# Norm weights and adaLN shifts applied along rows, and splits of four chunks out of PSUM, in a fused transformer kernel

## Chip, cores and metric

One Trainium2 chip, one core. The time is device microseconds of one execution, median of several. Lower is better.

## What is computed

512 tokens of width 1024 in float32 pass through two layers of a first block (a sparse-attention mixer "NSA", an MLP, a sliding-window mixer "SWA", a second MLP, each with adaptive norm) and then through a second block (a hybrid mixer, cross-attention to 256 memory tokens, a convolutional FFN). The parts that matter here are the norms in front of each of these and how their results enter the next projection:

```python
def modulate(h, shift, scale):
    return h * (1 + scale[:, None, :]) + shift[:, None, :]

mod = cond @ ada_w[i] + ada_b[i]
sh1, sc1, g1, sh2, sc2, g2 = jnp.split(mod, 6, axis=-1)
h = modulate(rms_norm(x, norm_g[i, 0]), sh1, sc1)      # mixer input
y = nsa_mixer(h, ...) or swa_sink_mixer(h, ...)
x = x + (1 + g1)[:, None, :] * rms_norm(y, norm_g[i, 1])
h = modulate(rms_norm(x, norm_g[i, 2]), sh2, sc2)      # MLP input
y = squared_relu_mlp(h, ...)
x = x + (1 + g2)[:, None, :] * rms_norm(y, norm_g[i, 3])
# second block: plain weights, no shift
h = rms_norm_2(x, norm_mix_w);   x = x + hybrid_mixer(h, ...)
h = rms_norm_2(x, norm_xattn_w); m = rms_norm_2(mem, norm_mem_w)
x = x + memory_cross_attention(h, m, ...)
h = rms_norm_2(x, norm_ffn_w);   x = x + conv_ffn(h, ...)
return rms_norm_2(x, norm_final_w)
```

So six times a normed and weighted x becomes the h of the next stage, three times (after NSA, the first MLP and SWA) with a shift, three times (after the second MLP, the hybrid mixer and cross-attention) without; the memory's norm is the seventh, and is done twice, since its keys and its values are made at different times.

## The kernel before

Matmuls keep float32 accuracy by three products of reduced-precision parts: `mm3` (L127) adds high by high, high by low and low by high. Every operand therefore exists as a high part, which ACT makes by a copy (`split`, L96), and a low part, which DVE makes by subtraction (L97). Weights come from HBM in 512 KB pieces through SP's queue (`load`, L77, in program order), into three buffers `st`, and `wload` (L113) splits each into `wh` and `wl` (five buffers each). The adaLN matrices are loaded by the same queue as tiles `ad` and multiplied on DVE (L341); when the eight jobs of one part are done, `ada_part` finishes its coefficient [128, 8], eight columns of 128 features (L357 for shifts, L363 for scales).

x lies with tokens on the partitions, four blocks of 128. The matmuls need h with features on the partitions: eight chunks of 128 features by 512 tokens. `norm_T` (L296) makes it. For each token block DVE multiplies the first half of x by the reciprocal norm r (L300) and ACT the second half (L301); TensorE transposes the eight 128 x 128 pieces (L448) into a PSUM bank "t"; for each chunk ACT (L315 without shift, L317 with) or DVE (L319, L321) takes it out of PSUM with the chunk's weight and shift as one scalar per partition, into a tile `nt`; then it is split into hH (ACT) and hL (DVE). `NB` gives the engine of each bank. h has eight tiles hH and eight tiles hL of [128, 512]; the same buffers carry the last attention outputs (`h_tile`), which the out-projection reads, and then the new h.

`norm_T` is called by `y_last` (after an out-projection with adaLN: NSA, first MLP, SWA, second MLP), by `to_h` (after those without) and by `mem_norm` (memory). In `y_last` a gate row `cb` is multiplied along the row (L931, L933 and the like); such a row comes from `along_rows` (L324): a coefficient [128, 8] is stored by POOL's DMA queue to a 4 KB tile Rd in DRAM with features in order (L327), then read back as a broadcast to 128 partitions (L329). There are five of these: the four gates and the final norm's weight.

The order of instructions is set by a planner over the program: each engine has one in-order stream, in which work is placed when its data are expected. Only the loads of `load` are held to program order.

Of the kernel before, what the change touches and what calls it, by code (L numbers as in the profile page):

```python
# [18 lines left out]
NST, NXT, NXQ, NAT = 6, 4, 4, 8  # L19
NAD, NR = 1, 3  # L20
NW = 5
TSE = 'GG'
NB = 'AVAV'
ON_PE = (8, 0, 1, 10, 3, 5)
FIRST = 5
XB, XE = ("mm", "t"), "AVAVAVAV"
# [19 lines left out]
def body(nc, tc, A, out):  # L46
# [89 lines left out]

    def chunk_terms(w, h, cols, ks):
        wh, wl = w
        hh, hl = h
        return [(kc(wh, j), kc(wl, j), hh[k][:, cols], hl[k][:, cols]) for j, k in enumerate(ks)]  # L140

    def h_tile():
        return [hp.tile([128, 512], F32R, name=n, tag=n, bufs=8) for n in ("hH", "hL")]

    def new_h(n=512, pool_=None, tags=("hH", "hL"), bufs=8):
        p_ = hp if pool_ is None else pool_
        hh = [p_.tile([128, n], F32R, name=tags[0], tag=tags[0], bufs=bufs) for _ in range(8)]
        hl = [p_.tile([128, n], F32R, name=tags[1], tag=tags[1], bufs=bufs) for _ in range(8)]
        return hh, hl

    def late_order(nk, n):

# [142 lines left out]

    def norm_T(xs, Rs, to, h, c, a, b=None):  # L296

        w = 128 * len(xs)
        for x, r, t in zip(xs, Rs, to):
            V.tensor_scalar(t[:, :512], x[:, :512], r, None, op0=OP.mult)  # L300
            S.activation(t[:, 512:], x[:, 512:], AF.Copy, scale=r)  # L301
        nb = 512 // w
        for m0 in range(0, 8, nb):
            o = mm("t")
            for u in range(nb):
                for i, t in enumerate(to):
                    transpose(o[:, u * w + i * 128:u * w + i * 128 + 128], kc(t, m0 + u))
            on = NB[m0 // nb]
            for u in range(nb):
                m = m0 + u  # L310
                hh, hl, v, g = h[0][m][:, c], h[1][m][:, c], kc(o, u, w), a[:, m:m + 1]
                t = tmp("nt", [128, 256], bufs=4)[:, :w]
                if on == "A":
                    if b is None:
                        S.activation(t, v, AF.Copy, scale=g)  # L315
                    else:
                        S.activation(t, v, AF.Identity, bias=b[:, m:m + 1], scale=g)  # L317
                elif b is None:
                    V.tensor_scalar(t, v, g, None, op0=OP.mult)  # L319
                else:  # L320
                    V.tensor_scalar(t, v, g, b[:, m:m + 1], op0=OP.mult, op1=OP.add)  # L321
                split(hh, hl, t)

    def along_rows(col, t):  # L324

        d = dr.tile([8, 128], F32, name="Rd", tag="Rd", bufs=2)
        G.dma_start(d.rearrange("m p -> p m"), col)  # L327
        flat = d.rearrange("m p -> (m p)")
        G.dma_start(t, bass.AP(tensor=flat.tensor, offset=flat.offset, ap=[[0, 128], [1, 1024]]))  # L329
        return t  # L330


    nw = {n: w2nd[:, 8 * i:8 * i + 8] for i, n in enumerate(("mix", "xattn", "mem", "ffn", "final"))}
    mod = C("mod", [128, 96])

    ada_pool = [None, 1, "ad"]
# [46 lines left out]
    def mem_norm(p, mh):  # L383
        ts, rs = [], []
        for i in range(2):
            t = p.tile([128, 1024], F32, name="relu", tag="relu", bufs=NR)
            Q.dma_start(t, A["mem"][i])
            ss = tmp("ss", [128, 4], bufs=12)
            mean_sq(t, ss[:, :1])
            ts.append(t)  # L390
            rs.append(rcol(ss[:, :1], 1))
        norm_T(ts, rs, ts, mh, slice(0, 256), nw["mem"])

    def mem_keys(p, mh):
        for m in range(8):
# [161 lines left out]
    def nsa(h, a_out):  # L557
        full = slice(0, 512)
        with ExitStack() as pools:
# [238 lines left out]
            def attend(i, g2, a):  # L798
# [24 lines left out]
                if a == 1:  # L823
                    two(O[g2], [VC[:, 2 * g2 + u] for u in range(2)], (qs[i][1],) * 2, False, True)
                if a == 1 and i == 3:
                    hh, ll = h_tile()
                    split(hh, ll, O[g2])
                    a_out[0].append(hh)
                    a_out[1].append(ll)
                elif a == 1:  # L830
                    oo = p5.tile([128, 512], F32, name="oo", tag="oo", bufs=2)
                    S.activation(oo, O[g2], AF.Copy)
                    Q.dma_start(Od[i * 2 + g2], oo)
# [87 lines left out]
    def y_last(how, src, a, nk, y, acc, x, h, cb, an, bn):  # L921

        ss = [small4() for _ in range(4)]

        def evac(tb, n, o):
            c = WIDTHS[n]
            if not acc:
                mean_sq(o, ss[tb][:, n:n + 1])
                V.tensor_tensor(y[:, tb, c], o, cb[:, c], op=OP.mult)  # L929
            else:  # L930
                V.tensor_tensor(y[:, tb, c], y[:, tb, c], o, op=OP.add)  # L931
                mean_sq(y[:, tb, c], ss[tb][:, n:n + 1])
                V.tensor_tensor(y[:, tb, c], y[:, tb, c], cb[:, c], op=OP.mult)  # L933

        def done(tbs):
            s2 = []
            for tb in tbs:
                r = total(ss[tb])
                s2.append(small4())
                for n, c in enumerate(WIDTHS):  # L940
                    V.scalar_tensor_tensor(x[:, tb, c], y[:, tb, c], r, x[:, tb, c], op0=OP.mult, op1=OP.add)
                    mean_sq(x[:, tb, c], s2[-1][:, n:n + 1])
            norm_T([x[:, tb] for tb in tbs], [total(s) for s in s2], [y[:, tb] for tb in tbs], h, cols_of(tbs), an(), bn())
        how(src, a, nk, evac, done)

    def x_last(src, a, nk, x, then):
# [166 lines left out]
    def mlp(l, h, p, pa, x, y, hn, an, bn, mem):  # L1113
        for tb in range(4):
            G.dma_start(Xd[tb], x[:, tb])
        with ExitStack() as pools:
            for g in range(4):
# [4 lines left out]
                if g == 3:  # L1122
                    seven_ctx.close()
                    for tb in range(4):
                        G.dma_start(x[:, tb], Xd[tb])
                    cb = along_rows(need(l, 5), pools.enter_context(pool("along")).tile(
                        [128, 1024], F32, name="along", tag="along"))
                blocks = Blocks(pa, sp) if g in (1, 2) else None

                def src7(k, n, q, g=g):  # L1130
# [65 lines left out]
    def swa(h, p, pa, a_out):  # L1196
# [24 lines left out]
        def attend(j, q2):  # L1221
# [4 lines left out]
            for jj in range(0, 4, 2):  # L1226
# [14 lines left out]
                for k in (jj, jj + 1):  # L1241
                    n = 256 if k < 3 else 128
                    for u in range(2):
                        T.matmul(O[64 * u:64 * u + 64, 128 * k:128 * k + n], VV[:, k, j // 2],
                                 pt[u][:, 256 * (k - jj):256 * (k - jj) + n], start=k == 0, stop=k == 3,
                                 skip_group_check=True)
            hh, ll = a_tile(pa, 6) if j < 3 else h_tile()
            split(hh, ll, O)
            a_out[0].append(hh)
            a_out[1].append(ll)  # L1250
# [65 lines left out]
    def hybrid(h, p, pa, a_out):  # L1316
# [142 lines left out]
                outs[hd] = ob  # L1459

        def combine(hd):
            hh, ll = a_tile(pa, 7) if hd < 3 else h_tile()
            G.tensor_tensor(outs[hd], outs[hd], gate[hd], op=OP.mult)
            split(hh, ll, outs[hd])
            a_out[0][4 + hd], a_out[1][4 + hd] = hh, ll
# [28 lines left out]
    def cross(h, p, pa, a_out):  # L1494
# [12 lines left out]
        def attend(hd):  # L1507
# [30 lines left out]
            for dc in range(2):  # L1538
                o = mm("o")
                mm3(o, [(kc(vv[j][0], 2 * hd + dc), kc(vv[j][1], 2 * hd + dc), pt[j][0], pt[j][1]) for j in range(2)])  # L1540
                hh, ll = a_tile(pa, 6) if hd < 3 else h_tile()
                split(hh, ll, o)
                a_out[0].append(hh)
                a_out[1].append(ll)
# [66 lines left out]
    def whole():  # L1611
# [7 lines left out]
        x = xp.tile([128, 4, 1024], F32, name="x", tag="x")  # L1619

        def to_h(hn, w):
            return lambda tbs, rs: norm_T([x[:, tb] for tb in tbs], rs, [tmp("xn", [128, 1024], bufs=4) for _ in tbs],
                                          hn, cols_of(tbs), w)

        def out_of(name):
# [207 lines left out]
```

## Time and profile before

| | us |
|---|---|
| median of three runs | 2063.8 (2063.65 to 2072.12) |
| the profiled execution | 2068.99 |
| its span in the profile | 2067.2 |
| TensorE busy | 1970.3 (95%) |
| DVE busy | 1351.1 (65%) |
| ACT busy | 971.9 (47%) |
| POOL busy | 295.4 (14%) |

The span runs from the first to the last instruction that the profile shows. Busy shares are means over stages of very different kinds; the mean granted clock of TensorE is 0.977 of full speed. A row of a view of groups gives line, engine, operation, output and inputs by name, the count, busy time, the mean duration, and the idle time of the engine just ahead of it with what ended it. A row of waits gives who waited, for what, and how long. All instants are microseconds from the start of the span.

### The profile page before, as it was taken

To read this page: it belongs to the slowest core of one execution; us is meant where nothing else is said; L and a number is where in the kernel's file an instruction comes from. 1 tells how busy PE (TensorE), PEld (TensorE's weight loads), DVE (VectorE), ACT (ScalarE), POOL (GpSimd) and SP (SyncE) were. 2 spreads that over 40 slices of the span, in tenths; PEclk is the share of its full clock that TensorE was granted. 3 is DMA by queue.
4 is the path that set the end of the run, shared out by engine and by line. 5 is a ranking of instruction groups with operands and counts; after the bars stand their busy time and mean duration, and the time that the engine had idled before them with its cause. 6 is when DMAs were issued, how large, how long until landed. Compare 5 with 4: busy or idle time off the path is not lost.

```text
span 2067.2 us, 27292 instructions
## 1 busy us (share of the span) xinstructions
PE 1970.3 (95%) x9878; PEld 1600.6 (77%) x9878; DVE 1351.1 (65%) x2608; ACT 971.9 (47%) x1846; POOL 295.4 (14%) x251
## 2 busy tenths in 40 slices
PE   8979999989989998999889999999999999999998
PEld 7766565678767887876678888888888888788786
DVE  6768777386677776776652676367635656767854
ACT  5346566363243434655543444455535454444442
POOL 0401211012022120320020211202010000301200
PEclk9999999999999999999989999999999999999999
DMA  7765331356935475540422343333322333252331
GB/s 296 227 191 152 102 114 49 112 195 205 273 122 174 166 240 147 171 135 20 173 93 92 117 148 123 133 112 117 98 72 68 106 114 107 85 155 92 102 103 51
DMA packets 89224, 276.64 MB, mean 134 GB/s; under 512 B 14209, under 2 KB 17217, under 8 KB 89090
## 3 DMA queue, kind: packets, MB, share of 16 engines
q1 hardware_dynamic: 82802, 258.68, 39.4%
q0 software_dynamic: 4432, 13.63, 2.0%
q10 hardware_dynamic: 1856, 2.59, 0.5%
q8 instruction: 78, 1.28, 0.3%
q14 instruction: 56, 0.46, 0.1%
HBM read 246.58 MB, written 10.51 MB: 124 GB/s over the span
## 4 chain that ended last, share of the span: by engine, by line
PE 44%; DVE 3%; ACT 1%; DMA 1%; issue 1%; POOL 0%; DVEq 0%; POOLq 0%; ACTq 0%
PE mm L130 10%; PE mm L131 10%; PE mm L132 10%; PE o L130 3%; PE o L132 3%; PE o L131 3%; DVE wl L97 1%; PE t L130 1%; PE t L131 1%; PE t L132 1%; PE t L448 1%; DMA st<-in_w_xq_dram 0%; ACT wh L96 0%; PE o L1445 0%; DMA st<-in_w_fdown_dram 0%
## 5 line engine op out<-in xcount | busy, mean ns | idle before, releaser
L130 PE MATMUL mm<-hH,wh 128*128 128x512 f32 (+1 forms) x1456 | 519.9, 360 | 22.3 <-ACT wh L96 14.1
L131 PE MATMUL mm<-hL,wh 128*128 128x512 f32 (+1 forms) x1456 | 520.8, 359 | 2.1 <-DVE hL L97 2.1
L97 DVE TENSOR_TENSOR wl<-st,wh 128x1024 fp32r<-128x1024 f32 x287 | 360.7, 1261 | 247.4 <-ACT wh L96 246.9
L132 PE MATMUL mm<-hH,wl 128*128 128x512 f32 (+1 forms) x1456 | 519.6, 359 | 2.4 <-DVE wl L97 2.4
L96 ACT ACTIVATE wh<-st 128x1024 fp32r<-128x1024 f32 (+1 forms) x295 | 308.7, 1052 | 447.8 <-PE mm L131 197.4
L130 PEld LDWEIGHTS mm<-hH,wh 128*128 128x128 f32 x1456 | 277.9, 192 | 63.9 <-ACT wh L96 15.1
L131 PEld LDWEIGHTS mm<-hL,wh 128*128 128x128 f32 x1456 | 279.0, 192 | 41.4 <-DVE hL L97 2.5
L132 PEld LDWEIGHTS mm<-hH,wl 128*128 128x128 f32 x1456 | 278.6, 192 | 41.7 <-DVE wl L97 3.0
L341 DVE SCALAR_TENSOR_TENSOR ad<-ad,cs 128x1024 f32<-128x1024 f32 x90 | 114.8, 1279 | 74.0 <-DMA ad<-in_ada_w_dram 73.7
L130 PE MATMUL o<-wh,aH 128*128 128x512 f32 x284 | 113.2, 399 | 10.0 <-DVE y L929 5.7
L130 PE MATMUL mm<-wh,aH 128*128 128x512 f32 x300 | 118.2, 396 | 4.0 <-ACT aH L96 4.0
L131 PE MATMUL mm<-wl,aH 128*128 128x512 f32 x300 | 118.5, 395 | 0.0
L132 PE MATMUL mm<-wh,aL 128*128 128x512 f32 x300 | 115.4, 393 | 0.0
L132 PE MATMUL o<-wh,aL 128*128 128x512 f32 x284 | 112.7, 397 | 0.5 <-DVE aL L97 0.5
L131 PE MATMUL o<-wl,aH 128*128 128x512 f32 x284 | 112.5, 396 | 0.0
L448 PEld LDWEIGHTS t<-pack,P 128*128 128x128 f32 x436 | 47.9, 143 | 63.4 <-issue 48.7
L1141 POOL TENSOR_TENSOR relu<-relu 128x512 f32<-128x512 f32 x32 | 54.7, 1711 | 277.7 <-ACT relu L1140 211.6
L448 PE MATMUL t<-pack,P 128*128 128x128 f32 x436 | 77.3, 292 | 10.6 <-ACT P L692 8.1
L753 ACT ACTIVATE P<-P,m 128x128 f32<-128x128 f32 (+3 forms) x128 | 70.9, 556 | 28.8 <-DVE m L751 27.3
L764 PE MATMUL o<-PT,VV 128*64 128x512 f32 (+3 forms) x256 | 79.3, 454 | 0.1
L96 ACT ACTIVATE aH<-relu 128x256 fp32r<-128x256 f32 (+2 forms) x70 | 41.4, 593 | 80.4 <-POOL relu L1150 43.0
L1150 POOL TENSOR_TENSOR relu<-relu 128x256 f32<-128x256 f32 (+1 forms) x46 | 57.2, 1254 | 146.6 <-ACT relu L1149 126.3
(467 smaller groups left out, 3651.9 us busy)
## 6 DMA issues: line engine op xcount, KB each, us to landing
ad<-in_ada_w_dram SPq DMA_DIRECT2D x90, 512.0 KB, 4.8
st<-in_w_up_dram SPq DMA_DIRECT2D x64, 512.0 KB, 3.6
st<-in_w_down_dram SPq DMA_DIRECT2D x56, 512.0 KB, 3.6
st<-in_w_fup_dram SPq DMA_DIRECT2D x44, 512.0 KB, 3.6
st<-in_w_fdown_dram SPq DMA_DIRECT2D x22, 512.0 KB, 3.5
st<-in_w_nsa_dram SPq DMA_DIRECT2D x16, 512.0 KB, 6.3
x<-in_w_down_dram SPq DMA_DIRECT2D x16, 512.0 KB, 3.9
raw<-in_w_down_dram SPq DMA_DIRECT2D x16, 512.0 KB, 3.8
```

The costliest lines, as they stand in the source:

```text
L96: S.activation(h, src, AF.Copy)
L97: eng.tensor_tensor(l, src, f(h), op=OP.subtract)
L130: T.matmul(o, ah, bh, start=start and i == 0, stop=False, **kw)
L131: T.matmul(o, ah, bl, start=False, stop=False, **kw)
L132: T.matmul(o, al, bh, start=False, stop=stop and i == n - 1, **kw)
L341: V.scalar_tensor_tensor(w, w, 1.0, cs, op0=OP.mult, op1=OP.mult, accum_out=mod[:, j:j + 1])
L448: T.transpose(o, i, ident[:n, :n] if n < 128 else ident)
L753: S.activation(pq, pq, AF.Exp, bias=m[:, qb:qb + 1], scale=-1.0, accum_out=d[:, qb:qb + 1])
L764: T.matmul(o[64 * u:64 * u + 64], vs[u], ps_[u], start=start, stop=stop, skip_group_check=True)
L1141: G.tensor_tensor(r, r, r, op=OP.mult)
L1150: G.tensor_tensor(r, r, r, op=OP.mult)
```

## The change

The norm's weight and shift are no longer applied per chunk after the transposes but along the rows ahead of them: DVE multiplies x by r and by the row of weights in one operation per half, and adds the row of shifts in a second operation where there is one. The banks of transposed pieces are then split straight out of PSUM, all chunks of a bank in one ACT and one DVE operation, with no `nt` tile. For that h becomes two tiles of four chunks for hH and two for hL. The rows are brought as the gates' are, by a store to DRAM and a broadcast load; the store is now a function `to_dram`. The memory weight's store stands at the start of the program (`Md`), and its row is loaded in both of its norms. In `y_last` the coefficients are asked for at its start and not at the first norm; in the MLP that precedes, at its last quarter.

```diff
-NB = 'AVAV'
...
-    def h_tile():
-        return [hp.tile([128, 512], F32R, name=n, tag=n, bufs=8) for n in ("hH", "hL")]
-
-    def new_h(n=512, pool_=None, tags=("hH", "hL"), bufs=8):
+    spare = []
+
+    def h_tile(n):
+
+        if n == 0:
+            spare[:] = [hp.tile([128, 2048], F32R, name=q, tag=q, bufs=2) for q in ("hH", "hL")]
+        return [kc(t, n, 512) for t in spare]
+
+    def new_h(n=512, pool_=None, tags=("hH", "hL")):
+
         p_ = hp if pool_ is None else pool_
-        hh = [p_.tile([128, n], F32R, name=tags[0], tag=tags[0], bufs=bufs) for _ in range(8)]
-        hl = [p_.tile([128, n], F32R, name=tags[1], tag=tags[1], bufs=bufs) for _ in range(8)]
-        return hh, hl
+        big = [[p_.tile([128, 4 * n], F32R, name=q, tag=q, bufs=2) for _ in range(2)] for q in tags]
+        return [[kc(b[m // 4], m % 4, n) for m in range(8)] for b in big] + [big]
...
     def norm_T(xs, Rs, to, h, c, a, b=None):
 
+        for x, r, t in zip(xs, Rs, to):
+            for n in (slice(0, 512), slice(512, 1024)):
+                V.scalar_tensor_tensor(t[:, n], x[:, n], r, a[:, n], op0=OP.mult, op1=OP.mult)
+                if b is not None:
+                    V.tensor_tensor(t[:, n], t[:, n], b[:, n], op=OP.add)
         w = 128 * len(xs)
-        for x, r, t in zip(xs, Rs, to):
-            V.tensor_scalar(t[:, :512], x[:, :512], r, None, op0=OP.mult)
-            S.activation(t[:, 512:], x[:, 512:], AF.Copy, scale=r)
         nb = 512 // w
...
-            on = NB[m0 // nb]
-            for u in range(nb):
-                m = m0 + u
-                hh, hl, v, g = h[0][m][:, c], h[1][m][:, c], kc(o, u, w), a[:, m:m + 1]
-                t = tmp("nt", [128, 256], bufs=4)[:, :w]
...
-                split(hh, hl, t)
-
-    def along_rows(col, t):
-
-        d = dr.tile([8, 128], F32, name="Rd", tag="Rd", bufs=2)
+            hh, hl = (t[m0 // 4].rearrange("p (m t) -> p m t", m=4)[:, m0 % 4:m0 % 4 + nb, c] for t in h[2])
+            split(hh, hl, o.rearrange("p (m t) -> p m t", m=nb))
+
+    def to_dram(col, tag="Rd", bufs=2):
+        d = dr.tile([8, 128], F32, name=tag, tag=tag, bufs=bufs)
         G.dma_start(d.rearrange("m p -> p m"), col)
+        return d
+
+    def along_rows(col, t, d=None):
+
+        if d is None:
+            d = to_dram(col)
         flat = d.rearrange("m p -> (m p)")
         G.dma_start(t, bass.AP(tensor=flat.tensor, offset=flat.offset, ap=[[0, 128], [1, 1024]]))
         return t
 
+    def row(name, col):
+        return along_rows(col, tmp("row_" + name, [128, 1024], bufs=1))
...
+    mem_w = to_dram(nw["mem"], "Md", 1)
...
-        norm_T(ts, rs, ts, mh, slice(0, 256), nw["mem"])
+        norm_T(ts, rs, ts, mh, slice(0, 256), along_rows(None, tmp("row_mem", [128, 1024], bufs=1), mem_w))
...
     def y_last(how, src, a, nk, y, acc, x, h, cb, an, bn):
 
         ss = [small4() for _ in range(4)]
+        if callable(an):
+            an, bn = (None if t is None else row("ab"[i], t) for i, t in enumerate((an(), bn())))
...
-            norm_T([x[:, tb] for tb in tbs], [total(s) for s in s2], [y[:, tb] for tb in tbs], h, cols_of(tbs), an(), bn())
+            norm_T([x[:, tb] for tb in tbs], [total(s) for s in s2], [y[:, tb] for tb in tbs], h, cols_of(tbs), an, bn)
...
-                    cb = along_rows(need(l, 5), pools.enter_context(pool("along")).tile(
-                        [128, 1024], F32, name="along", tag="along"))
+                    rp = pools.enter_context(pool("along"))
+                    cb, an, bn = (None if t is None else along_rows(t, rp.tile([128, 1024], F32, name=n, tag=n))
+                                  for n, t in (("along", need(l, 5)), ("row_a", an()), ("row_b", bn())))
...
         def to_h(hn, w):
-            return lambda tbs, rs: norm_T([x[:, tb] for tb in tbs], rs, [tmp("xn", [128, 1024], bufs=4) for _ in tbs],
+            w = row("a", w)
+            return lambda tbs, rs: norm_T([x[:, tb] for tb in tbs], rs, [tmp("xn", [128, 1024], bufs=XN) for _ in tbs],
                                           hn, cols_of(tbs), w)
```

The other lines of the diff pass a number to `h_tile`, so that two or four attention outputs share one large tile.

## Rows read from the trace of the kernel before

**Rows 1.** The page, part 1: busy us, share of the span, instructions.
```profile
PE 1970.3 (95%) x9878; PEld 1600.6 (77%) x9878; DVE 1351.1 (65%) x2608; ACT 971.9 (47%) x1846; POOL 295.4 (14%) x251
```

**Rows 2.** Waits in 440 to 460 and 1030 to 1050: us in total, times, longest.
```profile
PE mm L130 <- ACT wh L96: 5.8, 1, 5.8
...
PE mm L130 <- ACT wh L96: 8.3, 1, 8.3
```

**Rows 3.** Waits in 121 to 138, then in 805 to 831.
```profile
ACT wh L96 <- DMA st<-in_phi_w_dram: 9.1, 2, 8.9
...
PE t L448 <- ACT P L692: 8.1, 1, 8.1
...
ACT wh L96 <- DMA st<-in_w_mk_dram: 10.4, 1, 10.4
...
PE t L448 <- DVE y L300: 5.0, 1, 5.0
```

**Rows 4.** DMA issues (KB, median us to landing) in 119-122, 122-129 and 803.5-808.
```profile
st<-in_phi_w_dram SPq DMA_DIRECT2D x1, 512.0 KB, 4.6
Rd<-coef POOLq DMA_DIRECT2D x1, 4.0 KB, 10.9
...
st<-in_phi_w_dram SPq DMA_DIRECT2D x3, 512.0 KB, 10.8
...
st<-in_w_mk_dram SPq DMA_DIRECT2D x3, 512.0 KB, 15.2
Rd<-pack POOLq DMA_DIRECT2D x1, 4.0 KB, 15.8
```

**Rows 5.** Windows: from:to, length, busy PE, PEld, DVE, ACT, POOL; PEclk, DMA share, GB/s.
```profile
122.50:131.50 9.00, 7.24 (x32) 5.17 (x30) 5.59 (x9) 3.83 (x4) 0.00 (x0) 1.00 0.46 36
132.60:142.80 10.20, 4.92 (x14) 4.05 (x15) 6.19 (x10) 5.46 (x7) 0.00 (x0) 0.50 0.85 308
0.00:40.00 40.00, 33.26 (x126) 28.12 (x127) 27.00 (x62) 23.04 (x34) 0.88 (x5) 1.00 0.95 371
517.50:526.00 8.50, 8.50 (x39) 7.04 (x38) 2.37 (x3) 0.48 (x1) 0.00 (x0) 1.00 0.68 68
535.00:547.00 12.00, 12.00 (x55) 9.94 (x54) 9.23 (x16) 3.28 (x5) 0.00 (x0) 1.00 0.94 328
```

**Rows 6.** Groups by line, ACT then DVE: busy us, mean ns, idle before.
```profile
L301 ACT ACTIVATE y<-x,rc_r 128x512 f32<-128x512 f32 x16 | 11.3, 717 | 2.2 <-DVE rc_r L288 1.3 <-DVE rc_s L286 0.9
L317 ACT ACTIVATE nt<-t,mod,coef 128x256 f32<-128x256 f32 (+1 forms) x32 | 14.1, 508 | 5.7 <-PE t L448 3.9 <-DVE hL L97 1.7
L96 ACT ACTIVATE hH<-nt 128x256 fp32r<-128x256 f32 (+1 forms) x128 | 39.3, 362 | 13.0 <-DVE nt L321 7.7 <-DVE nt L319 2.3 <-PE o L131 2.3
...
L321 DVE TENSOR_SCALAR nt<-t,coef,mod 128x256 f32<-128x256 f32 (+1 forms) x32 | 14.1, 471 | 1.5 <-PE t L448 1.4
L97 DVE TENSOR_TENSOR hL<-nt,hH 128x256 fp32r<-128x256 f32 (+1 forms) x128 | 42.8, 367 | 14.3 <-ACT hH L96 13.9
```

**Rows 7.** The same view, nearest rows for the new operations.
```profile
L96 ACT ACTIVATE xTh<-t 128x512 fp32r<-128x512 f32 x8 | 4.3, 597 | 7.7 <-PE t L448 7.7
...
L941 DVE SCALAR_TENSOR_TENSOR x<-y,rc_r,x 128x512 f32<-128x512 f32 x32 | 22.5, 747 | 0.2
L933 DVE TENSOR_TENSOR y<-y,along 128x512 f32<-128x512 f32 x16 | 10.5, 690 | 1.1 <-ACT relu L294 0.9
L97 DVE TENSOR_TENSOR xTl<-t,xTh 128x512 fp32r<-128x512 f32 x8 | 5.1, 683 | 6.2 <-ACT xTh L96 6.2
```

**Rows 8.** Store, row loads, first and last coefficient: start us, us, what, idle before.
```profile
120.24 0.95 POOL L327 DMA_DIRECT2D Rd<-coef  x1 [18.53 <-DVE coef L363]
...
L329 POOL DMA_DIRECT2D along<-Rd x5: 530/583/615, 367.3 to 1699.2; - x5
...
185.68 0.16 DVE L363 SCALAR_TENSOR_TENSOR coef<-mod,pack 128x8 f32<-128x8 f32 x1
...
758.48 0.16 DVE L357 TENSOR_TENSOR mod<-mod,pack 128x8 f32<-128x8 f32 x1
```

More of the change, by code (lines that the diff above doesn't have):

```diff
@@ L21 @@
 NW = 5
+XN = 4
 TSE = 'GG'
-NB = 'AVAV'
 ON_PE = (8, 0, 1, 10, 3, 5)
@@ L138, in chunk_terms @@
         wh, wl = w
-        hh, hl = h
+        hh, hl = h[:2]
         return [(kc(wh, j), kc(wl, j), hh[k][:, cols], hl[k][:, cols]) for j, k in enumerate(ks)]
-    def h_tile():
-        return [hp.tile([128, 512], F32R, name=n, tag=n, bufs=8) for n in ("hH", "hL")]
-    def new_h(n=512, pool_=None, tags=("hH", "hL"), bufs=8):
+    spare = []
[4 more added lines that the diff above has]
+    def new_h(n=512, pool_=None, tags=("hH", "hL")):
         p_ = hp if pool_ is None else pool_
-        hh = [p_.tile([128, n], F32R, name=tags[0], tag=tags[0], bufs=bufs) for _ in range(8)]
-        hl = [p_.tile([128, n], F32R, name=tags[1], tag=tags[1], bufs=bufs) for _ in range(8)]
-        return hh, hl
+        big = [[p_.tile([128, 4 * n], F32R, name=q, tag=q, bufs=2) for _ in range(2)] for q in tags]
+        return [[kc(b[m // 4], m % 4, n) for m in range(8)] for b in big] + [big]
     def late_order(nk, n):
@@ L307, in norm_T @@
                     transpose(o[:, u * w + i * 128:u * w + i * 128 + 128], kc(t, m0 + u))
-            on = NB[m0 // nb]
-            for u in range(nb):
-                m = m0 + u
-                hh, hl, v, g = h[0][m][:, c], h[1][m][:, c], kc(o, u, w), a[:, m:m + 1]
-                t = tmp("nt", [128, 256], bufs=4)[:, :w]
[L313 to L321, printed above, removed]
-                split(hh, hl, t)
-    def along_rows(col, t):
-        d = dr.tile([8, 128], F32, name="Rd", tag="Rd", bufs=2)
+            hh, hl = (t[m0 // 4].rearrange("p (m t) -> p m t", m=4)[:, m0 % 4:m0 % 4 + nb, c] for t in h[2])
+            split(hh, hl, o.rearrange("p (m t) -> p m t", m=nb))
+    def to_dram(col, tag="Rd", bufs=2):
+        d = dr.tile([8, 128], F32, name=tag, tag=tag, bufs=bufs)
         G.dma_start(d.rearrange("m p -> p m"), col)
+        return d
+    def along_rows(col, t, d=None):
+        if d is None:
+            d = to_dram(col)
         flat = d.rearrange("m p -> (m p)")
@@ L825, in attend @@
                 if a == 1 and i == 3:
-                    hh, ll = h_tile()
+                    hh, ll = h_tile(g2)
                     split(hh, ll, O[g2])
@@ L1246, in attend @@
                                  skip_group_check=True)
-            hh, ll = a_tile(pa, 6) if j < 3 else h_tile()
+            hh, ll = a_tile(pa, 6) if j < 3 else h_tile(q2)
             split(hh, ll, O)
@@ L1461, in combine @@
         def combine(hd):
-            hh, ll = a_tile(pa, 7) if hd < 3 else h_tile()
+            hh, ll = a_tile(pa, 7) if hd < 3 else h_tile(0)
             G.tensor_tensor(outs[hd], outs[hd], gate[hd], op=OP.mult)
@@ L1540, in attend @@
                 mm3(o, [(kc(vv[j][0], 2 * hd + dc), kc(vv[j][1], 2 * hd + dc), pt[j][0], pt[j][1]) for j in range(2)])
-                hh, ll = a_tile(pa, 6) if hd < 3 else h_tile()
+                hh, ll = a_tile(pa, 6) if hd < 3 else h_tile(dc)
                 split(hh, ll, o)
```

## The prediction, made before the changed kernel was run

> **What bounds the kernel now.** I read the page first: TensorE (PE) is busy for 1970.3 us, 95% of the span [rows 1]. The profiled execution took 2068.99 us (its span of 2067.2 and 1.8 around it), 5.2 above the median of 2063.8; the sum below is made against 2068.99 and moved by −5.2 at the end. So PE's idle 97 us and the stretches at half clock behind its longer gaps are all that a change off PE can win, while anything that lengthens a gap is paid in full. So the second view was the waits of PE in each stretch, the third what held the engine that PE waited for, the fourth the DMA issues of that moment.
>
> Two kinds of gap matter. **Norm gaps**: at the end of the NSA projection PE waits 5.8 us and at the end of SWA 8.3 us for a weight split (wh, L96) [rows 2]. ACT works in order, and that split stands behind the norm's scalings, evacuations and hH copies. **Store gaps**: near 130 us PE waits 8.1 us for ACT, which had waited 9.1 us for a weight from DMA; near 825 PE waits 5.0 us for the norm's y (L300, DVE), after ACT had waited 10.4 us for a w_mk load [rows 3] and DVE for ACT's half of that split. Both stand behind one kind of transfer: the 4 KB store Rd<-coef of `along_rows` (L327), 1024 elements of 4 bytes each going to its own place. It takes 10.9 us to land, one sent directly behind another 15.8; a weight load that took 4.6 us just before takes 10.8 beside it, and w_mk loads take 15.2 [rows 4]. In 122.5 to 131.5 the DMA engines are 46% busy and move 36 GB/s [rows 5]. A few KB therefore take the transfers of a whole core away for 8 to 10 us.
>
> The rule of the Trainium skill that speaks against these stores is in "DMA: Bandwidth & Descriptors", section "Rules for kernel authors": a non-contiguous last dimension becomes one descriptor per element. The 36 GB/s agree in direction. The same page, "Anatomy of one DMA — SWDGE (gpsimd) path", fits a DMA as 2.0 us plus bytes over 436 GB/s, some 2 us for 4 KB by its figures; the trace shows 10.9 and 15.8 us. By that fit the stores would cost nothing.
>
> **The change: norm sites.** In a site with a shift (three of six; 512 tokens), before: ACT has 4 × 0.717 us (L301), a third of 14.1 us (L317) and a sixth of 39.3 us (hH), 2.9 + 4.7 + 6.6 = 14.2 us. DVE has a third of 14.1 us (L321), a sixth of 42.8 us (hL) and four scalings shorter than ACT's, 4.7 + 7.1 + about 2 = 13.8 us [rows 6]. After: ACT keeps eight splits of a bank. The nearest row is xTh<-t, also out of a PSUM bank: 8 × 0.597 = 4.8 us. DVE has eight scalar_tensor_tensor at 0.747 (L941), eight adds at 0.690 (L933) and eight subtractions at 0.683 (xTl): 17.0 us; without a shift 11.4 [rows 7]. So ACT is relieved of 9.4 us a site and DVE gets 3.2 more with a shift, 2 or so less without.
>
> What of this PE sees: a weight split no longer queues on ACT behind some 4 us per token block. But the first transposes of a block wait for two scalings and two adds in one chain on DVE (2 × 0.747 + 2 × 0.690 = 2.9 us) where they waited for one scaling beside ACT's (0.7). The wl half of the split runs on DVE and stands behind that. So of the 5.8 us I take 3, of the 8.3 I take 5, and 1 from the other sites: −9. Bounds: −20 (both gaps and the 5.0 of site two gone) and +5 (DVE's extra 3.2 us shown in each shift site, the half of it beside PE). Behind the 8.1 us gap the clock stands at 0.50, the lower of its two levels, for 10.2 us, in which PE does what needs half as long at the upper one [rows 5]: half of such a stretch, up to 5 us, is lost per gap. Shorter norm gaps give back 3 us. Sum −12.
>
> The loss of `nt` buffers and h in two tiles a half costs 0 to 3: chunks 4 to 7 of the new h share a tile with inputs of the last out-projection matmuls and may wait for these; transposes are issued behind these matmuls on PE anyway. I take 0. The 11 further row loads are broadcasts of 512 KB from POOL's queue, with contiguous rows; loads of that size land in 4.6 us [rows 4] and their data are wanted long after, so 0, at most 2 each where POOL's squares stand behind a load that waits for its store.
>
> **The change: stores.** Every row that is newly applied needs such a store: two per layer's scale and shift twice (six), the mixer, cross-attention, FFN weights (three), and the memory weight at the program's start: ten more beside five. When do they go out? POOL waited only for the coefficient (idle 18.5 us until L363) and sent the store at once [rows 8]; the store of the final norm weight, whose data are constant, left directly behind the last coefficient's near 804 us [rows 4], though its load comes at 1699.2 [rows 8]. So stores leave in program order as soon as the data are there, not when the row is wanted. The six coefficients are ready between 185.7 and 758.5 us [rows 8] (the four between at 234, 537, 554 and 735). The constant ones join the two at 804. Priced one by one:
> - 804 us: five stores in a row instead of two. The second of the two, sent 1 us behind the first, lands after 15.8 us where a lone one takes 10.9 [rows 4], so each further one adds 15.8 + 1 − 10.9 = 5.9 us; three are 18 us more of blackout, to about 839. Weight splits on ACT and DVE stand ahead of the norm that PE waits for. Bounds 0 (weights already loaded) and 18; part of the loads still moves by the GB/s above, so +14.
> - start: in 0 to 40 us DMA is 95% busy at 371 GB/s and PE is short of work by 6.7 us already [rows 5]. A blackout of 9 us there: 0 to 9, I take +6.
> - 537 and 554: at 535 to 547 DMA is 94% busy at 328 GB/s with PE at 100% [rows 5]: no slack to win a blackout back. The store at 512 left PE without a gap (8.50 of 8.50 us busy while 68 GB/s moved [rows 5]), out of weights loaded ahead; two more within 17 us find fewer of them. 0 to 16, I take +8.
> - 186 and 234: attention, few weights; 0 to 8, +2. 735 and 758: 0 to 10, +3.
> - clock behind the new gaps: two to four gaps of over 5 us at up to 5 us, 0 to 12, +5.
> Sum +38, bounds 0 and 73; 3.8 us for each of ten. The five stores of before left gaps of 8.1 and 5.0 us [rows 3], 2.6 per store, and with up to 5 for the clock behind each 4.6: the value lies between.
>
> Net: +38 − 12 = +26, so 2068.99 + 26 = 2095, less 5.2: **2090 us**.
>
> **Rivals.** (A) *Stores spread*: the pool of row copies in DRAM has two places; if a store has to wait for an earlier row's load, the cluster at 804 does not grow and stores move to where rows are read. For it: bufs=2 in the code. Against: the final store left 895 us ahead of its load with two others not yet read. Price: of the +38 the start, 186 and some of the rest, +20; 2069 + 20 − 12 − 5 = 2072. Within 0.5%, or just not. (B) *Blackouts hidden*: each of them falls where weights are ahead, as that at 512 did, which left PE no gap. It decides if the w_mk stage and the start run on weights loaded ahead; then only the norm's −12 is left: 2069 − 12 − 5 = 2052, faster by 0.6%. For it: five weight buffers (NW), and the 8.50 of 8.50 us above. Against: both gaps of [rows 3] arose with only one or two stores. (C) *DVE takes ACT's place*: DVE's 2.9 us chain ahead of the transposes and later out-projection sums eat the norm gain wholly while stores cost as forecast: +38 + 5 = +43, 2107. It decides if PE's waits at the sites name the new scalings. (D) *A store costs by its bytes*, and the loads beside it are late for another reason, the bunching of SP's loads there: as B, 2052. Against: two places of [rows 4] with different loads, the same lateness. The fit of the Trainium skill named above ("DMA: Bandwidth & Descriptors", "Anatomy of one DMA — SWDGE (gpsimd) path") would be this case.
>
> **How the numbers follow.** Forecast (stores when ready, blackouts bite) 0.50; C 0.12; A 0.10; B and D together 0.28 (0.26 and 0.02), of which 0.22 beyond 0.5%. 0.5% (10 us) is about what a measurement of this kernel can tell from no change. Faster: 0.22, within 0.5%: 0.13 (0.07 of A, 0.06 of B), slower 0.65 (the forecast, C, 0.03 of A). The range takes B in at 2050 and C with a larger cluster at 2118; the forecast's own range is 2074 to 2118.
>
> **What would show it.** Right: fifteen Rd stores, five of them in a row near 804 us with loads of over 15 us behind them and DMA under 70 GB/s until about 840; PE waits of 10 to 20 us more in 805 to 850; loads of over 10 us near 537 and 554; ACT's busy time down by some 60 us, DVE's up by 5 or so; at the norm sites no PE wait on wh over 4 us. Wrong: stores that land in 3 us, or that leave right before their loads; PE gaps at the stores as before; or PE waits at the sites for the new scalings longer than 5 us.

## The result, and the profile after

The changed kernel takes 2125.7 us (2120.9 to 2130.1) against 2063.7: 1.030 times the time before, 95% interval 1.027 to 1.034. The forecast had the direction, 2090, but the time lies beyond the range of 2050 to 2118, and the loss of 62 us is more than double the 26 that were worked out. The profiled execution took 2120.9 us, 52 more than that of before.

Engines first: the page's part 1 of the changed kernel, the line that answers to [rows 1].

```profile
PE 1983.0 (94%) x9878; PEld 1608.8 (76%) x9878; DVE 1361.0 (64%) x2500; ACT 917.4 (43%) x1658; POOL 307.3 (15%) x272
```

ACT is relieved by 54 us and DVE has 10 more, about as worked out (60 and 5). No engine has become the bound by its sum. TensorE is busy for 12.7 us more with the same 9878 matmuls: its mean granted clock is 0.966 where it was 0.977, and with a lower level at half the upper one, as [rows 5] show it, that makes by estimate some 145 us of the span at the lower level in place of 95. The rest of the 52 us is in waits. To place the loss, the table below sets the start of the n-th matmul of TensorE in one trace against that in the other; where the difference grows, time is lost. Its rows are single records, and the loss between two rows is the difference of their last columns.

```
n      before   changed   later by
150      43.9      49.0       5.1   behind the store at the start
750     187.9     193.4       5.4
900     216.6     228.9      12.3   behind the store at 192
1800    404.7     417.0      12.3
2250    480.2     491.4      11.2   first norm (NSA) passed
2550    544.8     556.0      11.2
2850    633.8     653.0      19.2   behind the stores at 546 and 570
3300    735.8     755.0      19.2
3600    805.6     842.0      36.3   behind the stores at 759 and 786
4050    871.2     928.0      56.8   five stores at 838 to 842, and the first MLP's norm
4650    990.5    1050.0      59.6
5100   1078.4    1129.5      51.1   SWA's norm passed
9750   2029.7    2081.6      51.9
```

The stores are where they were expected, one at the start, each of the others when its data were ready, and five in a row; the row of five came at 838 and not at 804, because 34 us had been lost by then. DMA issues of the changed kernel (KB, median us to landing), in 837.5 to 843, then in 545 to 552, which answer to [rows 4]; then two windows (busy PE, PEld, DVE, ACT, POOL, clock, DMA share, GB/s), which answer to [rows 5]:

```profile
st<-in_w_mk_dram SPq DMA_DIRECT2D x2, 512.0 KB, 18.5
Rd<-pack POOLq DMA_DIRECT2D x4, 4.0 KB, 21.1
...
st<-in_w_up_dram SPq DMA_DIRECT2D x2, 512.0 KB, 10.9
```

```profile
546.50:557.00 10.50, 10.50 (x48) 8.71 (x47) 5.55 (x8) 1.06 (x1) 0.86 (x1) 1.00 0.81 185
839.00:866.00 27.00, 18.72 (x128) 17.28 (x126) 9.46 (x21) 5.46 (x10) 3.60 (x5) 0.92 0.83 85
```

For 27 us the core gets 85 GB/s, and PE is busy for 18.7 of them. What PE waits for behind the stores stands in the waits of the changed kernel (us in total, times, longest), in 195 to 215, 560 to 595, 775 to 812 and 838 to 880:

```profile
PE mm L751 <- DVE m L754: 6.8, 1, 6.8
DVE ad L344 <- DMA ad<-in_ada_w_dram: 6.7, 2, 6.5
...
ACT relu L1146 <- DVE ad L344: 18.5, 2, 11.0
DVE ad L344 <- DMA ad<-in_ada_w_dram: 17.9, 9, 8.1
PE mm L130 <- ACT relu L1146: 11.8, 2, 6.8
...
DVE ad L344 <- DMA ad<-in_ada_w_dram: 12.6, 6, 8.6
...
PE t L451 <- DVE relu L305: 9.0, 1, 9.0
...
ACT wh L96 <- DMA st<-in_w_mk_dram: 13.3, 2, 12.3
PE mm L130 <- ACT ke L403: 9.2, 1, 9.2
```

Only the last pair is the way that the forecast described, a weight that comes late. In the first three, the late transfer is an adaLN tile (`ad`), which TensorE does not need at all. In attention DVE works in order, and the maximum m that PE waits for stands behind the multiply of the late tile. In the MLP the adaLN tiles share three buffers with the activations (`ada_pool[:] = [p, NR, "relu"]`, L1629), so that a late tile keeps a relu from starting, and PE waits for the bank which that relu would free. Near 800 it is the norm of the memory, whose tiles lie in the same buffers: it stands behind a late `ad` in DVE's order, and PE waits 9.0 us to transpose its result.

Last the norms: the changed kernel's groups by line, which answer to [rows 6], and what is left of the wait of [rows 2] among PE's waits in 440 to 465.

```profile
L305 DVE SCALAR_TENSOR_TENSOR y<-x,rc_r,row_a 128x512 f32<-128x512 f32 x32 | 22.5, 747 | 0.1
L307 DVE TENSOR_TENSOR y<-y,row_b 128x512 f32<-128x512 f32 x24 | 15.6, 683 | 0.0
L97 DVE TENSOR_TENSOR hL<-t,hH 128x512 fp32r<-128x512 f32 x48 | 32.0, 684 | 22.1 <-ACT hH L96 21.9
L96 ACT ACTIVATE hH<-t 128x512 fp32r<-128x512 f32 x48 | 27.7, 594 | 40.0 <-PE t L451 37.6 <-PE o L131 2.2
```

```profile
PE t L451 <- DVE y L307: 1.8, 1, 1.8
PE mm L130 <- ACT wh L96: 1.7, 1, 1.7
```

The operations cost what the nearest rows said, 0.747, 0.683, 0.684 and 0.594 us [rows 7], and the wait for wh is down from 5.8 to 1.7 us, with a new gap of 1.8 for y ahead of it. Yet the table shows 1 us won behind NSA, 8 behind SWA, and 20 lost around the first MLP's end. What of that is stores and what is norms, the profile alone does not tell; the experiments do.

### The profile page after: what moved, and what is told of

It reads as the page before. It is cut to its first block, busy times and chain, and to the rows that moved or that the text cites. A ratio compares the mean times of both kernels' runs of the same rounds, so it can differ in the third digit from the quotient of the medians.

```text
span 2119.1 us, 26994 instructions
## 1 busy us (share of the span) xinstructions
PE 1983.0 (94%) x9878; PEld 1608.8 (76%) x9878; DVE 1361.0 (64%) x2500; ACT 917.4 (43%) x1658; POOL 307.3 (15%) x272
## 3 DMA queue, kind: packets, MB, share of 16 engines
q1 hardware_dynamic: 82802, 258.68, 39.7%
## 4 chain that ended last, share of the span: by engine, by line
PE 51%; DVE 7%; DMA 7%; issue 3%; ACT 2%; POOL 0%; SPq 0%; DVEq 0%; ACTq 0%; POOLq 0%
PE mm L131 11%; PE mm L132 11%; PE mm L130 11%; DMA ad<-in_ada_w_dram 3%; PE o L130 3%; PE o L131 3%; PE o L132 3%; DVE wl L97 3%; PE t L451 2%; PE t L130 1%; PE t L131 1%; PE t L132 1%; DMA st<-in_w_mk_dram 1%; PE o L1250 1%; DMA st<-in_w_fdown_dram 1%
## 5 line engine op out<-in xcount | busy, mean ns | idle before, releaser
L130 PEld LDWEIGHTS mm<-hH,wh 128*128 128x128 f32 x1456 | 279.0, 193 | 66.5 <-ACT relu L1146 12.7
L130 PEld LDWEIGHTS mm<-wh,aH 128*128 128x128 f32 x300 | 57.9, 193 | 22.3 <-ACT relu L1155 5.0
L96 ACT ACTIVATE aH<-relu 128x256 fp32r<-128x256 f32 (+2 forms) x70 | 41.3, 594 | 76.6 <-POOL relu L1156 39.7
```

What stands on the lines that cost most here:

```text
L96: S.activation(h, src, AF.Copy)
L130: T.matmul(o, ah, bh, start=start and i == 0, stop=False, **kw)
```

## The experiments

Times are compared as a difference to the kernel before, timed on the same chip in the same sitting: 2064.3 for the stores alone, the wide stores and the constant rows; 2065.2 for the three parts of the norms and for ACT's queue; 2059.9 for the others. The planner orders every kernel anew, so that a few us of any difference can come from another order.

**Stores alone.** Into the kernel before, at the places of the program where the changed kernel has them:

```diff
+    def spare_store(col, tag="Rx", bufs=2):
+        d = dr.tile([8, 128], F32, name=tag, tag=tag, bufs=bufs)
+        G.dma_start(d.rearrange("m p -> p m"), col)
...
+    spare_store(nw["mem"], "Md", 1)
...
```

> The kernel before, with the ten additional stores of element-wise rows alone (memory weight at the start, six coefficients, mixer, cross-attention and FFN weights), written to DRAM and never read; the norm sites are as before. Theory 1 (the stores' blackouts make the whole loss): between the landmarks of the changed kernel's trace the stretches behind stores lost 5 + 7 + 10 + 17 + 19 = 58 us, so about 2063.7 + 58 = 2122, range 2105 to 2130, and five Rd stores in a row near 840 with loads of over 20 us. Theory 2 (the new chain of DVE operations at the norm sites delays the transposes and the weight splits behind them; the late loads only coincide): 2063 to 2075.

Measured 2111.9 us (2104.1 to 2117.9), +47.6 (interval 41 to 53): in the range of theory 1 and far from that of theory 2, but 14 short of the changed kernel's +62. The three stores of weights came at 786 to 787, directly behind the last shift's at 785, and not near 840; that they have a tag of their own is the likely reason, and was not tried. Waits of this kernel in 775 to 830, and its DMA issues in 783 to 792:

```profile
DVE ad L346 <- DMA ad<-in_ada_w_dram: 16.5, 6, 11.1
...
ACT relu L1160 <- DVE ad L346: 13.5, 3, 8.2
ACT relu L294 <- DMA relu<-in_mem_dram: 13.2, 2, 12.3
...
PE mm L130 <- ACT relu L1160: 12.3, 2, 10.0
...
PE t L453 <- DVE relu L300: 8.5, 1, 8.5
```

```profile
st<-in_w_down_dram SPq DMA_DIRECT2D x1, 512.0 KB, 20.4
Rx<-pack POOLq DMA_DIRECT2D x3, 4.0 KB, 20.6
```

It is the same path by way of the relu buffers, and the memory's norm is late again, with the norms untouched. The stores are shown to cost some 48 us by themselves.

**All stores in runs of 512 bytes.** The column is turned on TensorE first, so that the store has eight contiguous runs; in the changed kernel and, for its five stores, in the kernel before:

```diff
-        G.dma_start(d.rearrange("m p -> p m"), col)
+        b = mm("o")[:8, :128]
+        T.transpose(b, col, ident)
+        r = const.tile([8, 128], F32, name="rt", tag="rt", bufs=1)
+        V.tensor_copy(r, b)
+        G.dma_start(d, r)
```

> The changed kernel, with every column of coefficients first turned by a PE transpose into eight partitions of 128, copied to SBUF by DVE and then stored as eight runs of 512 bytes; all fifteen stores and the memory weight's. Theory 1: the 58 us go, and of the kernel before's own five stores the gaps of 8.1, 4.1 and 5 to 6 us with the clock behind them, some 18 to 26; 2125.7 - 58 - 18 = 2050, range 2035 to 2056; stores land in 2 to 3 us and no load beside them takes over 7 outside the front. Theory 2: 2100 to 2125, stores quick but PE gaps at the norm sites as they are.

> The kernel before, with its five stores made in eight runs of 512 bytes (PE transpose, DVE copy, store). Theory 1: its PE gaps of 8.1 near 130, 4.1 at 618 and 5 to 6 at 821 to 830 go, with the lower clock behind them: 2063.7 - 18 to 26 = 2038 to 2046. Theory 2: these gaps have another cause and stay: 2060 to 2066.

Measured 2045.0 us (2040.9 to 2051.0) for the changed kernel and 2037.2 (2035.0 to 2037.7) for the kernel before: −19.3 and −27.1 to the kernel before as it was. A store now lands in 1.6 us where DMA is quiet and in 7.6 at most (DMA issues of the changed kernel with wide stores, 364 to 371):

```profile
Rd<-rt POOLq DMA_DIRECT2D x3, 4.0 KB, 1.6
```

and in the kernel before the waits of [rows 3] near 130 and 825 are gone, as theory 1 said (the time is 1 us below its range). The edit moves the stores too: the turn is work of TensorE and DVE that the planner places, and the first store of this kernel leaves at 365.3 where it left at 120.2. So five stores in pieces of 4 bytes cost the kernel before 27 us against wide ones that leave later; what the pieces alone cost is shown further down. But with the stores out of the way the changed kernel is the slower of the two by 7.8 us, where the forecast's norm part said 12 faster. Theory 1 is the larger part, not the whole.

**Constant rows from the inputs.** The weights of the norms that have no shift are read as rows from an input array; no store at the start, one in place of five near 840.

```diff
-    mem_w = to_dram(nw["mem"], "Md", 1)
+    nw = {n: n for n in ("mix", "xattn", "mem", "ffn", "final")}
...
+        if isinstance(col, str):
+            d = A["nrow_" + col]
```

> The changed kernel, with the five constant rows (memory, mixer, cross-attention, FFN and final weights) read as rows straight from the inputs, so without the store at the start and four of the five near 840; the ten stores of coefficients stay as they are, 4 bytes at a time. Theory 1: the 5 us at the start and 14 to 24 us near 840 go: 2125.7 - 5 - 19 = 2102, range 2093 to 2107. Theory 2: within 5 us of the changed kernel, 2120 to 2130.

Measured 2106.2 us (2104.0 to 2109.4), 19.5 less than the changed kernel. In the two traces the start gives back 5 and the stretch from the 3600th to the 3900th matmul 14. The terms for the start (+6) and for the row of five (+14) were about right.

**Which part of the norms.** Two rivals were left: the row-wise operations ahead of the transposes, or the tiles of four chunks. With wide stores, (a) the kernel before with only h in large tiles (`h_tile` and `new_h` of the change, `norm_T` as it was); (b) the changed kernel without the adds, so that its result lacks the shift; (c) row-wise norms behind NSA and SWA only (where `a` is a row; columns take the old way):

```diff
(b)
-                    V.tensor_tensor(t[:, n], t[:, n], b[:, n], op=OP.add)
+                    pass
(c)
     def norm_T(xs, Rs, to, h, c, a, b=None):
 
...
+        if a.shape[-1] == 8:
+            for x, r, t in zip(xs, Rs, to):
+                V.tensor_scalar(t[:, :512], x[:, :512], r, None, op0=OP.mult)
+                S.activation(t[:, 512:], x[:, 512:], AF.Copy, scale=r)
...
+            return
```

> The kernel before with its stores made in eight runs of 512 bytes (2037.2 us), and h in two tiles of four chunks, each for hH and hL; norms as before, chunk by chunk out of PSUM, with the weight as one scalar per partition. Theory N1 (the changed norms lose at the first MLP's end because the row-wise multiply and add queue on DVE ahead of the transposes): the shared tiles cost nothing, 2034 to 2041. Theory N2 (a matmul on one chunk now waits for the whole tile of four): 2042 to 2048, with the PE gaps of the kernel with all stores wide near 814 to 865.

> The changed kernel with all stores in runs of 512 bytes (2045.0 us), without the 24 adds of the shift rows (the shift is left out of the result at the three sites that have one; its rows are still stored and loaded). Theory N1: 24 x 0.69 = 16.6 us less on DVE, the first transposes at the first MLP's end come 3 to 4 us earlier, and some 5 to 8 us of PE's loss there go: 2036 to 2041. Theory N2: 2043 to 2047.

> Stores in runs of 512 bytes, h in two large tiles, and the row-wise norm only behind the NSA and SWA out-projections; the other norms as before, out of PSUM chunk by chunk. From the two traces with wide stores: row-wise norms win some 2 us behind NSA and 10 behind SWA and lose some 12 at the first MLP's end and the SWA stage behind it. Theory N1 (the loss belongs to that site alone, the wins stand by themselves): 2037.2 - 2 to - 12 = 2025 to 2035. Theory N2, or wins that only make up time lost before: 2036 to 2045.

Measured 2035.1 (2029.6 to 2041.9), 2021.8 (2020.5 to 2023.0) and 2023.2 us (2020.4 to 2025.6): −30.2, −43.5 and −42.0. The large tiles cost nothing; N2 falls. The 24 adds, 15.5 us of DVE work, cost 24 us, three times what N1 said and beyond its range; some 4 of these stand at the program's start in this pair of traces, ahead of any norm, so 20 is the better figure. Without them row-wise norms win 16 us over the kernel before with wide stores (again some 5 of it at the start in these traces). And row-wise norms where (c) keeps them are worth 12 against (a), which has the large tiles too, and 15 against the kernel before with wide stores; (c) came out 2 us below N1's range.

Set against each other as in the table above, the traces with and without the adds differ by 8 us behind NSA and 6 at the first MLP's end. How an add of 0.68 us costs so much is seen on DVE at the latter. First the changed kernel with wide stores (timeline of DVE, then of PE: start, us, what), then the two scalings of the same blocks in the kernel before with wide stores:

```profile
800.98 1.41 DVE L305 SCALAR_TENSOR_TENSOR y<-x,rc_r,row_a 128x512 f32<-128x512 f32 x2
802.31 1.22 DVE L97 TENSOR_TENSOR wl<-st,wh 128x1024 fp32r<-128x1024 f32 x1
...
803.59 0.67 DVE L307 TENSOR_TENSOR y<-y,row_b 128x512 f32<-128x512 f32 x1
...
804.84 1.22 DVE L97 TENSOR_TENSOR wl<-st,wh 128x1024 fp32r<-128x1024 f32 x1
...
810.31 1.41 DVE L305 SCALAR_TENSOR_TENSOR y<-x,rc_r,row_a 128x512 f32<-128x512 f32 x2
811.63 2.73 DVE L950 SCALAR_TENSOR_TENSOR x<-y,rc_r,x 128x512 f32<-128x512 f32 x4
814.28 1.29 DVE L307 TENSOR_TENSOR y<-y,row_b 128x512 f32<-128x512 f32 x2
...
815.02 0.88 PE L455 MATMUL t<-pack,y 128*128 128x128 f32 x6 [1.35 <-DVE y L307]
```

```profile
802.10 0.48 DVE L300 TENSOR_SCALAR y<-x,rc_r 128x512 f32<-128x512 f32 x1
...
805.98 0.48 DVE L300 TENSOR_SCALAR y<-x,rc_r 128x512 f32<-128x512 f32 x1
```

A block's four operations are not done in 2.9 us one after the other. Between its multiply and its add stand weight splits and the residuals of the next blocks, in DVE's one order; the second block's y is ready at 815.6 where it was at 806.5 (its ACT half came sooner still), and its transposes with it; 4.3 us of that were lost ahead of its multiply already. All transposes of this site then end at 832.7, 39.7 us after the first residual update, against 31.0 in the kernel before with wide stores and 35.0 without the adds. Behind it the SWA stage starts with less work to cover its own chain.

What the lateness costs is a gap and the clock behind it. Windows (as above: length, busy PE and so on, clock), behind NSA: 45 us from 8 us ahead of the first residual update and the 8 us after them, first without and then with the adds; then 85 us from the same point at the first MLP's end, in the kernel before, without and with the adds, all with wide stores:

```profile
396.50:441.50 45.00, 45.00 (x276) 39.96 (x275) 34.26 (x78) 26.32 (x60) 5.88 (x8) 1.00 0.55 196
441.50:449.50 8.00, 8.00 (x69) 8.00 (x68) 8.00 (x10) 3.39 (x8) 2.93 (x3) 1.00 0.39 152
...
401.00:446.00 45.00, 41.27 (x240) 35.63 (x239) 34.23 (x85) 23.52 (x57) 5.99 (x8) 1.00 0.44 152
446.00:454.00 8.00, 7.54 (x40) 7.24 (x41) 8.00 (x9) 3.66 (x5) 0.00 (x0) 0.59 0.97 358
...
786.00:871.00 85.00, 83.30 (x584) 77.30 (x584) 68.52 (x160) 53.01 (x117) 25.10 (x20) 1.00 0.58 172
771.50:856.50 85.00, 79.08 (x543) 73.44 (x542) 62.38 (x133) 42.89 (x92) 23.76 (x18) 0.96 0.51 149
785.00:870.00 85.00, 75.46 (x515) 70.40 (x514) 63.42 (x130) 40.55 (x83) 24.99 (x18) 0.94 0.49 144
```

Behind NSA TensorE has no gap without the adds. With them it lacks 4 us of busy time, and then runs for 8 us at a mean granted clock of 0.59, which by estimate takes some 3 us more: about the 8 us lost there. At the first MLP's end the adds explain only a part. Row-wise norms lose there 15 us to the kernel before, and 9 without the adds (start times of the 3600th and the 4500th matmul); why they lose these 9 was not tried.

Behind SWA the same change wins. Waits of PE in 995 to 1025, in the kernel before with wide stores, then in the changed kernel with wide stores:

```profile
PE mm L130 <- ACT wh L96: 8.9, 1, 8.9
```

```profile
PE t L455 <- DVE y L307: 3.7, 1, 3.7
```

There PE has run out of other work in both, and a wait for ACT's queue of 8.9 us gives way to one of 3.7 for the add.

**Adds on POOL.** In the changed kernel with wide stores:

> The changed kernel with all stores in runs of 512 bytes (2045.0 us), the 24 adds of the shift rows on POOL in place of DVE. Theory N1 (the loss is DVE's queue): DVE has 16.6 us less; POOL takes some 1.7 us per add of 128x512, a chain of 3.4 us per block that runs beside DVE's other work: 2028 to 2040. If the chain's length counts and not DVE's queue: 2045 to 2055.

```diff
-                    V.tensor_tensor(t[:, n], t[:, n], b[:, n], op=OP.add)
+                    G.tensor_tensor(t[:, n], t[:, n], b[:, n], op=OP.add)
```

Measured 2049.5 us (2043.6 to 2055.6), −10.4 to its kernel before, so 9 behind the adds on DVE. POOL's row of the groups by line:

```profile
L307 POOL TENSOR_TENSOR y<-y,row_b 128x512 f32<-128x512 f32 x24 | 40.6, 1709 | 84.7 <-DVE y L305 84.7
```

N1 put the loss on DVE's amount of work, and that falls: DVE is rid of all adds, and the kernel is slower. An add takes 1.71 instead of 0.68 us, and the transposes at the first MLP's end finish 46.2 us after the first residual. This fits the second theory: the time goes with how late y is ready, not with how busy DVE is.

**Both losses together.** The changed kernel with its stores as they are, without the adds (the edit of (b)):

> The changed kernel as it is, with stores of 4 bytes, without the 24 adds of the shift rows (the shift is left out of the result). If the two losses add up: 2125.7 - 16 to - 23 = 2102 to 2110. If the adds cost more while loads are late (the norm of the first MLP falls into the blackout near 840): 2090 to 2102. If late loads hide them: 2115 to 2126.

Measured 2091.8 us (2086.5 to 2100.1), +31.9: the adds cost 30 beside late loads, against 20 to 24 without these, a difference no larger than the intervals of these runs. In the two traces it is 8 behind NSA, 11 at the first MLP's end, 4 behind SWA, and some 6 at the stores at 570 to 620.

**What makes a store dear.** The changed kernel with its 4-byte stores on ACT's queue, and with 128 runs of 32 bytes on POOL's (which puts the rows' features in another order, so that the result is not the function's):

```diff
-        G.dma_start(d.rearrange("m p -> p m"), col)
+        S.dma_start(d.rearrange("m p -> p m"), col)
```

```diff
-        d = dr.tile([8, 128], F32, name=tag, tag=tag, bufs=bufs)
-        G.dma_start(d.rearrange("m p -> p m"), col)
+        d = dr.tile([128, 8], F32, name=tag, tag=tag, bufs=bufs)
+        G.dma_start(d, col)
```

> The changed kernel with its stores still in elements of 4 bytes, but issued from ACT's DMA queue in place of POOL's. Theory E (1024 elements of 4 bytes occupy the DMA engines whoever sends them): stores land in 9 us or more, loads beside them late, 2110 to 2130. Theory Q (POOL's queue is what stops the other transfers): landing in under 4 us and 2042 to 2060.

> The changed kernel with its stores on POOL's queue, but each partition's eight numbers kept together, 128 runs of 32 bytes in place of 1024 of 4 (the rows then come back in another order, so weights and shifts stand at other features). Theory E1 (a store costs by its number of runs): 10.9 us for 1024 against 1.5 to 4 for 8 leaves some 3 us for 128, loads beside it at most 2 us late: 2045 to 2058. Theory E2 (any run far under 512 bytes is as bad): landing in 8 us or more, 2095 to 2125.

Measured 2125.0 us (2118.3 to 2128.7) and 2046.3 (2042.7 to 2050.4): +59.7 and −13.6. DMA issues in 191 to 194 with ACT's queue, and in 225 to 235 and 775 to 790 (five at once) with runs of 32 bytes:

```profile
Rd<-coef ACTq DMA_DIRECT2D x1, 4.0 KB, 11.1
```

```profile
Rd<-mod POOLq DMA_DIRECT2D x1, 4.0 KB, 1.9
...
Rd<-pack POOLq DMA_DIRECT2D x4, 4.0 KB, 3.5
```

Windows behind the store at 192, from POOL's queue in the changed kernel, then from ACT's:

```profile
194.00:203.00 9.00, 7.27 (x39) 3.88 (x38) 5.85 (x15) 4.08 (x11) 1.88 (x2) 1.00 0.22 17
194.00:203.00 9.00, 8.21 (x43) 4.27 (x42) 4.94 (x14) 4.67 (x13) 1.88 (x2) 1.00 0.20 16
```

The same 4 KB take 11 us in 1024 pieces from either queue, and 1.9 in 128. Theories E and E1 hold. The stores of 32-byte runs leave when their data are ready, as the changed kernel's do, five in a row at 782 to 785; only their pieces differ, and the kernel is 75.6 us faster than the changed one, each against its kernel before. So it is the number of pieces that costs, and not the moment.

**A better version.** Kernel (c) with row-wise norms also at the sites without a shift, their rows read from the inputs:

```diff
                     an, bn = an_(), bn_()
+                    if bn is None:
+                        an = along_rows(an, rp.tile([128, 1024], F32, name="row_a", tag="row_a"))
```

> The kernel with rows at two sites (2023.2 us), with row-wise norms also at the three sites without a shift and for the memory, whose rows are read from the inputs and need no store; at the first MLP's end the norm stays chunk by chunk. Theory N1 (a row-wise norm without adds costs DVE no more than before and relieves ACT): 2015 to 2023. If these sites lose as the first MLP's did: 2026 to 2035.

Measured 2021.0 us (2018.0 to 2025.0), −38.9 against −42.0 for (c): no difference that these runs can tell. Both are faster than the kernel before, by some 2% (ratios 0.982, interval 0.979 to 0.985, and 0.980, 0.977 to 0.983), with all stores wide and the chunk-by-chunk norm kept at the first MLP's end.

## Why the prediction was right in direction and wrong in size

The account closes in three steps, each a difference of two kernels: stores +47.6; row-wise norms and large tiles without the adds −15.7 (2111.9 to 2091.8, each against its kernel before); the adds +30.1. Sum +62.0; it has to close, since the kernels are taken in a row, and each step is uncertain by 6 us or more. One row of the kernel before is needed below, from its waits in 533 to 563:

```profile
ACT relu L1140 <- DVE ad L341: 7.6, 1, 7.6
```

- **Stores leave when their data are ready**: right. Fifteen stores, five in a row; rival A (stores spread by two places in DRAM) did not happen.
- **A store takes DMA away for 8 to 10 us**: right, and of the two rules weighed, the one in the Trainium skill, "DMA: Bandwidth & Descriptors", "Rules for kernel authors" (one descriptor per element where the last dimension isn't contiguous; rearrange it), agrees with 11 us for 1024 pieces and 1.9 for 128. The fit in "Anatomy of one DMA — SWDGE (gpsimd) path" of that page of the Trainium skill, some 2 us by its figures, agrees with the contiguous stores (1.6 us) and not with these; rival D falls.
- **Their price, +38**: 47.6 measured. Start +6 (5 in the trace), 537 and 554 +8 (8 to 10) and the row of five +14 (14) were near. Mis-sized were 186 (+2 for it and 234; 7 in the trace) and 735 and 758 (+3, bound 10; 17). The first was priced by how few weights the stage needs, the second without a reason. What came late was adaLN tiles, which hold DVE's order in attention and the relu buffers in the MLP, and behind them the memory's norm; the coupling of `ad` to `relu` was to be read in L1629 and in the kernel before's own waits in 533 to 563 (the row above), and was not followed. Rival B (hidden) falls with the 47.6.
- **Clock behind the new gaps, +5, bounds 0 and 12**: too small, as far as known. TensorE's busy time rose by 12.7 us for the same matmuls. It was priced per gap at up to half of a stretch of 10.2 us, though TensorE was busy for 4.92 us of that stretch [rows 5]; the stretches at the lower level grew by some 50 us in sum, by the estimate above, more than two to four gaps make. What the clock cost by itself was not measured.
- **Norm sites, −12, bounds −20 and +5**: the step that failed. It measured +7.8 with quick stores and +14.4 beside late ones. ACT's relief was right, and with wide stores, row-wise norms without the adds win 16 us over the kernel before (some 5 of it at the program's start) and 13 over the one with large tiles. The adds were given 3.2 us of extra DVE work per site, with a share of it shown to PE; they cost 20 to 30. The chain of 2.9 us per block was summed as if its operations ran back to back, while in the planner's order weight splits and residuals stand between them; and a gap so made was priced without the lower clock behind it (0.59 behind NSA). Rival C, DVE in ACT's place, is nearest to what happened, at +7.8 to +14.4 where it put +5. Its test, "waits at the sites for the new scalings", was too narrow: a planner fills PE with other work, and the longest wait of PE for a new y in the changed kernel is 2.7 us.
- **Tiles of four chunks, 0**: right.

Not settled: why row-wise norms lose 9 us at the first MLP's end even without adds, where they win behind NSA and SWA. The thinner cover of the SWA stage is argued from the traces, not tried alone. Where the start of the program runs a few us earlier or later between kernels that are the same there, the cause was not looked for.

## What to carry to other kernels

Before a small transfer is added, count its contiguous runs, not its bytes, and see which loads it stands beside; if a column has to become a row, turn it on TensorE first. When an operation is put ahead of a chain's first step, price it by what the in-order engine will put between the links and by the clock behind the gap, not by its own duration. And follow a late transfer to every buffer and queue it shares, not only to the engine that reads it.

## What the runs showed of the hardware

A store of 4 KB in 1024 pieces of 4 bytes takes 11 us to land, whether POOL's or ACT's queue sends it, and lets the core's transfers fall to 36 GB/s in one place [rows 5] and to 17 (POOL's queue) and 16 (ACT's) in another; in 128 pieces of 32 bytes it takes 1.9, in eight of 512 bytes 1.6, where DMA is otherwise quiet. Beside loads, the longest for one sent by itself are 5.3 and 7.6. The median of four sent within 3 us is 21.1 and 3.5 us for the first two forms. A 128x512 add takes 1.71 us on POOL and 0.68 on DVE.
